# One stream for the recurrences of four token groups in a fused decoder block

## The chip, the core and the metric

The kernel runs on one core of a Trainium2 chip. A core has TensorE (PE; its weight loads are shown as PEld), VectorE (DVE), ScalarE (ACT), GpSimd (POOL) and a queue SP that issues the transfers here. Each works through its own instructions in order; semaphores tie them together. The metric is device time in microseconds for one execution; lower is better. Before the change the median of three runs is 2995.38 us.

## What is computed

One layer of a decoder on 2048 tokens of width 1024, in float32:

```python
u = rmsnorm(h, attn_pre_norm)
hq, hf, hi, hg, sq, sk, sv = split(u @ w_in)          # 7 parts of 512 columns
o_hg = rmsnorm(hgrn2_mix(hq, hf, hi, lb), hg_out_norm) * silu(hg)
o_sb = rmsnorm(stick_breaking_mix(sq, sk, sv), sb_out_norm)
h = h + rmsnorm(concat(o_hg, o_sb) @ w_out, attn_post_norm)
h = h + rmsnorm((silu(gate) * up) @ w_down, ffn_post_norm)   # gate, up from rmsnorm(h) @ w_gate_up
h = h + (p @ ple_proj) * sigmoid(h @ ple_gate)
```

`hgrn2_mix` is a gated linear recurrence with 4 heads: S_t = diag(f_t) S_(t-1) + (1 - f_t) v_t^T and o_t = S_t^T q_t, with a state of 128x128 per head. f comes from the logits `hf`, q from `hq` after silu, v is `hi`, and `hg` gates the output. `stick_breaking_mix` is strictly causal attention with 8 heads of width 64.

## The kernel before

The tokens are worked in four groups of 512 (`NG`, `GT`), each of four blocks of 128 (`TT`, `P`). Products that need more than one pass split both operands into a high and a low part and use three matmuls (`mm3`, L214 to L217).

**Two input projections per group.** `in_proj` (L335) computes either keys, queries and values of the attention (`KQV`, kind "a", 24 slots) or the four parts of the recurrence in the order hf, hq, hv, hg (`HG`, kind "b", 32 slots, eight for each part). A slot is two yields of the generator. Weights come through four raw buffers and a split (`weight`, L207; its DMA is L210, its subtraction L202). Results go to scratch in DRAM: `hf_s`, `hq_s`, `hv_s` and `hg_s` hold a group's logits, queries, values and gates (L367 to L381).

**The attention** is one stream for all groups (`attention`, L393), 320 units of two steps each. A unit makes scores into a `z` bank (L418), two sigmoids on ACT (L424, L425), a scan on DVE into `ring` (L439) and a product on POOL into `a` (L443). Four units later `a` is transposed (L451), split into `ah` (ACT, L454) and `al` (DVE, L456), and multiplied with the values (L467, L468).

**The recurrence** of one group is `hgrn(g)` (L501). For each of the four heads it has eleven steps, and two follow at the end, so 46 in all (`HG_STEPS`). A head's first step loads q (L508), logits z (L509), values v (L510) and gate (L511), makes pd and ks from z (L513 to L516), a tree of products on POOL (L524), and the first level. Seven level steps follow (`LEVELS`): matmuls into the bank `hg` (L533 for widths under 32, L544 for 32 and 64), a masked copy on DVE (L536), then a product of qp on POOL (L570) and one of ks on DVE (L572), both of which the next level needs. Then come a step that transposes ks (L577), one that multiplies it with v (L583) and forms the states on DVE (L587, sl in L593), and one that makes the output (L597, L598), adds its squares to `acc` on POOL (L605), multiplies with the gate (L606) and stores to `o_s` (L607). The last two steps sum `acc` over the head dimension with a matmul by ones (L613). There is one `hg` bank, and one buffer each for z, v, gate, pd, ks and qp; q has two. The state `hstate[h]` carries a head from group to group.

**What sets the order.** TensorE's order is the order of the program text, made by hand: `weave` (L51) advances a main stream slot by slot and steps the other streams as they fall due. The other engines and SP are ordered by a planner, which takes instructions by program order and its own estimate of when each becomes ready. `Rate` (L1181) deals out a number of steps of a stream over a number of slots. The phase says in which half of a slot steps are taken: 0, 1, or None for both.

The plan (L1221) lists seven projections that run after the first one: kind, group, units of attention, steps of recurrence. Before, each group's recurrence is a stream of its own, and an entry takes steps of one of them: n = 2 and 3 of group 0, n = 4 and 5 of group 1, n = 6 of group 2:

```python
("a", 1, units[0], 0), ("b", 0, 42, 0),
("a", 2, units[1] - 42, 21), ("b", 1, 48, 26),
("a", 3, 40, 21), ("b", 2, 52, 26), ("b", 3, 54, 42),
```

A group's recurrence is drained when n = 3 and n = 5 end. After n = 1 and n = 3 the last three slots are left to `in_u` (L306), which makes the operands of a later group and also uses the `hg` bank. Then come the output projections (`out_proj`, L642; 16 slots each). Beside that of group 0 run the last four steps of group 2 in the first two slots, and then group 3 at 46 steps over 30 slots, on into that of group 1. `out_load` (L620) loads a group's outputs from `o_s` for its output projection (DMA L625), and `post_mix` (L695) normalises and adds after it. The rest, a feed-forward with seven products in place of eight per block and the embedding gate, follows from about 1465 us on and is not touched.

Of the kernel before, what the change touches and what calls it, by code (L numbers as in the profile page):

```python
# [15 lines left out]
P = 128  # L16
# [74 lines left out]
def hybrid_block(  # L91
# [73 lines left out]
    def bank(tag):  # L165
        return ps.tile([P, 512], F32, tag=tag, name=tag, bufs=BANKS[tag])
# [334 lines left out]
    def hgrn(g):  # L501
        acc = None
        for h in range(HH):
# [6 lines left out]
            nc.sync.dma_start(v, hv_s[g][:, h * P:(h + 1) * P].rearrange("(c s) d -> s c d", s=P))  # L510
            nc.sync.dma_start(gate.rearrange("p c t -> p (c t)"), hg_s[g][h])  # L511
# [38 lines left out]
            for w in LEVELS:  # L550
                if w < BL:
                    level(qp, masks[w])
                else:
                    if w == BL:
                        b = bank("hg")
                        for i in range(0, P, BL):
                            nc.scalar.copy(score[i:i + BL, :, i:i + BL], small[i:i + BL])
                    blocks(b, w)
# [15 lines left out]
                yield  # L574
            kb = bank("hg")
# [15 lines left out]
            ob = bank("hg")  # L591
# [3 lines left out]
            yield  # L595
            for c in range(TT):
                nc.tensor.matmul(ob[:, c * P:(c + 1) * P], v[:, c, :], score[:, c, :], start=True, stop=False)  # L597
                nc.tensor.matmul(ob[:, c * P:(c + 1) * P], states[c], qp[:, c, :], start=False, stop=True)  # L598
# [597 lines left out]
    for i in range(WARM):  # L1196
# [26 lines left out]
        ("a", 2, units[1] - 42, 21), ("b", 1, 48, 26),  # L1223
        ("a", 3, 40, 21), ("b", 2, 52, 26), ("b", 3, 54, 42),
    ]
    hgs = [Stream(hgrn(g)) for g in range(NG)]
    spent = 0
    for n, (kind, g, att_n, hg_n) in enumerate(plan):
        slots = IN_A if kind == "a" else IN_B
        main = Stream(in_proj(g, us[g], KQV if kind == "a" else HG))  # L1230
        hg = {2: 0, 3: 0, 4: 1, 5: 1, 6: 2}.get(n)
        hg = hgs[hg] if hg is not None else idle
        tail = 3 if kind == "b" and g + 2 < NG else 0
        ra, rh = Rate(att_stream, 2, att_n, slots), Rate(hg, 1, hg_n, slots - tail)
        spent += att_n
        nxt = g + 2 if kind == "b" and g + 2 < NG else None
# [4 lines left out]
        if n in (3, 5):  # L1241
            hg.drain()
# [8 lines left out]
    r2 = Rate(hgs[2], 1, HG_STEPS - 42, 2)  # L1251
    r3 = Rate(hgs[3], 1, HG_STEPS, 2 * OP_SLOTS - 2)
# [9 lines left out]
    for g in range(NG - 1):  # L1262
# [3 lines left out]
        if g == 0:  # L1266
            weave(op, 2, rates.part(2), r2.part(2))
            hgs[2].drain()
            weave(op, OP_SLOTS - 2, rates.part(OP_SLOTS - 2), r3.part(OP_SLOTS - 2))
        elif g == 1:  # L1270
            weave(op, half, rates.part(half), r3.part(half), (pm, TT, 0))
            tu = Stream(turn(un_s[0], u_s[0], g_ffn, ["mm"], xt, ev))
            weave(op, half, rates.part(half), r3.part(half), (tu, 9, 0))
            hgs[3].drain()
# [95 lines left out]
```

## Time and profile before

| what | us |
|---|---|
| median of three runs (2991.2 to 3005.97) | 2995.38 |
| the profiled execution | 2993.67 |
| its span, first to last instruction | 2991.8 |
| TensorE busy in it | 2905.4 (97%) |
| first and last store of a recurrence head's output (L607) | 396.0, 1333.1 |
| DVE, ACT, POOL busy | 2067.2, 1581.7, 1404.1 |

The profile is of one execution. Busy time of an engine is the union of its instructions' times; matmuls are pipelined, so a busy TensorE is not one at its peak. "PE x <- DVE y" means that TensorE, at the instruction that writes x, waited for the DVE instruction that writes y. The granted clock (PEclk) is the share of the full TensorE clock; windows are in us from the span's start.

### The profile page before, as it was taken

How to read it: one execution, taken by the hardware profiler on the slowest of the kernel's cores; microseconds unless marked ns; L12 is line 12 of the kernel's file. 1: busy time of each engine (PE TensorE's matmuls, PEld its weight loads, DVE VectorE, ACT ScalarE, POOL GpSimd, SP SyncE). 2: the span in 40 equal slices, each digit the busy share in tenths (PEclk: the TensorE clock that was granted, in tenths of full speed). 3: DMA queues.
4: the chain of work that ended last, by engine and by line, in shares of the span. 5: the costliest groups of instructions: out<-in, count | busy, mean ns of one | idle time of the engine just before them, and what ended most of it. 6: DMA issues, size and time to landing. Idle time of an engine off the chain costs nothing.

```text
span 2991.8 us, 52684 instructions
## 1 busy us (share of the span) xinstructions
PE 2905.4 (97%) x18188; PEld 2424.4 (81%) x18188; DVE 2067.2 (69%) x2993; ACT 1581.7 (53%) x3182; POOL 1404.1 (47%) x1396
## 2 busy tenths in 40 slices
PE   9999999999999999898999999999999999999999
PEld 7788788878787887788878888788888888878777
DVE  3566667787777776766787787655877765656785
ACT  5666756676667666667533333455433323545542
POOL 3344556555556666765522211355622121456653
PEclk9999999999999999999999999999999999999999
DMA  7675665555445444457866787766965555677974
GB/s 223 206 221 156 181 183 165 147 175 165 142 138 162 148 134 133 158 189 260 288 185 209 252 289 259 244 206 209 346 201 163 166 176 176 208 218 234 326 250 162
DMA packets 469419, 602.27 MB, mean 201 GB/s; under 512 B 43168, under 2 KB 277664, under 8 KB 469152
## 3 DMA queue, kind: packets, MB, share of 16 engines
q1 hardware_dynamic: 469152, 598.91, 63.7%
q8 instruction: 143, 2.34, 0.3%
q14 instruction: 124, 1.02, 0.1%
HBM read 439.89 MB, written 158.86 MB: 200 GB/s over the span
## 4 chain that ended last, share of the span: by engine, by line
PE 47%; DMA 4%; POOL 3%; issue 3%; DVE 2%; ACT 1%; SPq 0%; POOLq 0%; ACTq 0%; DVEq 0%
PE mm L215 6%; PE mm L217 6%; PE mm L216 6%; PE z L217 4%; PE z L215 4%; PE z L216 4%; PE av L216 2%; PE av L215 2%; PE av L217 2%; PE tr L215 2%; PE tr L217 2%; PE tr L216 2%; POOL c L828 1%; POOL wl L821 1%; PE hg L217 1%
## 5 line engine op out<-in xcount | busy, mean ns | idle before, releaser
L820 ACT CAST wh<-wr 128x512 fp32r<-128x512 f32 x600 | 351.4, 618 | 477.3 <-PE mm L216 186.2
L821 POOL TENSOR_TENSOR wl<-wr,wh 128x512 fp32r<-128x512 f32 x256 | 366.9, 1440 | 471.5 <-ACT wh L820 416.8
L443 POOL TENSOR_TENSOR a<-be,ring 128x512 f32<-128x512 f32 (+2 forms) x320 | 320.0, 1000 | 417.1 <-DVE ring L439 394.4
L215 PE MATMUL mm<-uh,wh 128*128 128x512 f32 x1168 | 480.9, 412 | 3.5 <-DVE vv L358 2.4
L216 PE MATMUL mm<-ul,wh 128*128 128x512 f32 x1168 | 459.0, 393 | 3.9 <-DVE ul L821 2.3
L217 PE MATMUL mm<-uh,wl 128*128 128x512 f32 x1168 | 460.2, 394 | 0.0
L821 DVE TENSOR_TENSOR wl<-wr,wh 128x512 fp32r<-128x512 f32 x344 | 301.1, 883 | 183.9 <-ACT wh L820 173.3
L439 DVE TENSOR_TENSOR_SCAN ring<-z,ring,be 128x512 f32<-128x512 f32 x192 | 245.7, 1279 | 106.3 <-ACT z L425 103.8
L215 PE MATMUL mm<-wh,uh 128*128 128x256 f32 (+1 forms) x992 | 307.3, 310 | 0.9 <-DVE vv L358 0.9
L216 PE MATMUL mm<-wl,uh 128*128 128x256 f32 (+1 forms) x992 | 293.6, 296 | 0.6 <-POOL wl L821 0.6
L217 PE MATMUL mm<-wh,ul 128*128 128x256 f32 (+1 forms) x992 | 293.6, 296 | 0.0
L217 PEld LDWEIGHTS mm<-uh,wl 128*128 128x128 f32 x1168 | 220.4, 189 | 50.7
L215 PEld LDWEIGHTS mm<-uh,wh 128*128 128x128 f32 x1168 | 221.2, 189 | 46.2 <-issue 2.6
L216 PEld LDWEIGHTS mm<-ul,wh 128*128 128x128 f32 x1168 | 221.6, 190 | 44.8 <-DVE ul L821 2.7
L201 ACT CAST wh<-wr 128x512 fp32r<-128x512 f32 x288 | 178.3, 620 | 124.4 <-PE mm L216 71.7
L202 POOL TENSOR_TENSOR wl<-wr,wh 128x512 fp32r<-128x512 f32 x144 | 190.1, 1320 | 101.6 <-ACT wh L201 97.0
L424 ACT ACTIVATE be<-z 128x512 f32<-128x512 f32 (+2 forms) x320 | 171.0, 534 | 114.2 <-DVE z L422 66.8
L456 DVE TENSOR_TENSOR al<-tr,ah 128x512 fp32r<-128x512 f32 (+1 forms) x320 | 191.8, 599 | 50.5 <-ACT ah L454 48.6
L821 POOL TENSOR_TENSOR wl<-s,wh 128x512 fp32r<-128x512 f32 x44 | 73.0, 1661 | 300.7 <-ACT wh L820 263.6
L454 ACT CAST ah<-tr 128x512 fp32r<-128x512 f32 (+1 forms) x320 | 167.7, 524 | 87.8 <-PE tr L451 85.1
L215 PEld LDWEIGHTS mm<-wh,uh 128*128 128x128 f32 x992 | 191.4, 193 | 9.2 <-issue 1.1
L216 PEld LDWEIGHTS mm<-wl,uh 128*128 128x128 f32 x992 | 191.8, 193 | 6.5 <-POOL wl L821 1.1
(315 smaller groups left out, 7190.0 us busy)
## 6 DMA issues: line engine op xcount, KB each, us to landing
wr<-in_w_gate_up_dram SPq DMA_DIRECT2D x308, 256.0 KB, 3.8
wr<-in_w_in_dram SPq DMA_DIRECT2D x224, 256.0 KB, 3.2
wr<-hid_s SPq DMA_DIRECT2D x154, 256.0 KB, 3.3
wr<-in_w_down_dram SPq DMA_DIRECT2D x110, 256.0 KB, 3.6
wr<-wd_s SPq DMA_DIRECT2D x88, 256.0 KB, 3.2
kt<-k_s SPq DMA_DIRECT2D x80, 256.0 KB, 3.2
vt<-v_s SPq DMA_DIRECT2D x80, 256.0 KB, 3.4
wr<-h_s SPq DMA_DIRECT2D x80, 256.0 KB, 4.4
```

Of the source, the lines that this page charges most:

```text
L201: nc.scalar.copy(hi, src)
L202: (lo_engine or nc.gpsimd).tensor_tensor(lo, src, hi.bitcast(F32), op=ALU.subtract)
L215: nc.tensor.matmul(o, l[0], r[0], start=start, stop=False)
L216: nc.tensor.matmul(o, l[0], r[1], start=False, stop=False)
L217: nc.tensor.matmul(o, l[1], r[0], start=False, stop=stop)
L424: nc.scalar.activation(be[:, :n], z[:, :n], AF.Sigmoid, scale=0.125)
L439: nc.vector.tensor_tensor_scan(r[:, o:o + n][:, ::-1], z[:, :n][:, ::-1], be[:, :n][:, ::-1], init, op0=ALU.mult, op1=ALU.bypass)
L443: nc.gpsimd.tensor_tensor(a[:, :n], be[:, :n], r[:, o + 1:o + n + 1], op=ALU.mult)
L454: nc.scalar.copy(hi[:, lo_c:], tr[:, lo_c:])
L456: nc.vector.tensor_tensor(lo[:, lo_c:], tr[:, lo_c:], hi[:, lo_c:].bitcast(F32), op=ALU.subtract)
L820: nc.scalar.copy(hi, src)
L821: lo_engine.tensor_tensor(lo, src, hi.bitcast(F32), op=ALU.subtract)
```

## The change

The four streams become one, `hg`, that runs through the groups in order, 184 steps. The plan's entries take 24, 30, 20, 28 and 40 steps of it (142), wherever in the groups they fall, and the other 42 are dealt out over all 32 slots of the output projections of groups 0 and 1. So group 1 begins in n = 3, group 2 in n = 5 and group 3 at the end of n = 6, each while the projection that makes its own inputs is still under way. Within `hgrn`, the load of the values moves from the head's first step to the level of width 32 (its seventh step), and that of the gate to the step that transposes ks (its ninth); both now stand in the text behind the stores that they read. The bank for the output `ob` is asked for in the step that uses it. The entry n = 2 takes its steps in both halves of a slot (24 steps in 24 slots), n = 3 still in the second half alone. The drains after n = 3 and n = 5 go.

```diff
@@ -507,8 +507,6 @@
             q, z, v, gate = ht("q", 2), ht("z"), ht("v"), ht("gate")
             nc.sync.dma_start(q.rearrange("p c t -> p (c t)"), hq_s[g][h])
             nc.sync.dma_start(z.rearrange("p c t -> p (c t)"), hf_s[g][h])
-            nc.sync.dma_start(v, hv_s[g][:, h * P:(h + 1) * P].rearrange("(c s) d -> s c d", s=P))
-            nc.sync.dma_start(gate.rearrange("p c t -> p (c t)"), hg_s[g][h])
             pd, ks, qp = ht("pd"), ht("ks"), ht("qp")
             nc.scalar.activation(pd, z, AF.Sigmoid)
             nc.scalar.activation(ks, z, AF.Sigmoid, scale=-1.0)
@@ -552,6 +550,7 @@
                     level(qp, masks[w])
                 else:
                     if w == BL:
+                        nc.sync.dma_start(v, hv_s[g][:, h * P:(h + 1) * P].rearrange("(c s) d -> s c d", s=P))
                         b = bank("hg")
                         for i in range(0, P, BL):
                             nc.scalar.copy(score[i:i + BL, :, i:i + BL], small[i:i + BL])
@@ -572,6 +571,7 @@
                 nc.vector.tensor_tensor(
                     kv[:, :, 0, :], kv[:, :, 0, :], pv[:, :, 1:2].to_broadcast((P, n, w)), op=ALU.mult)
                 yield
+            nc.sync.dma_start(gate.rearrange("p c t -> p (c t)"), hg_s[g][h])
             kb = bank("hg")
             for c in range(TT):
                 nc.tensor.transpose(kb[:, c * P:(c + 1) * P], ks[:, c, :], ident)
@@ -588,11 +588,11 @@
                     st[:, c, :], states[-1], last[:, c:c + 1], sbk[:, c * P:(c + 1) * P],
                     op0=ALU.mult, op1=ALU.add)
                 states.append(st[:, c, :])
-            ob = bank("hg")
             s_last = ht("sl", shape=(P, P))
             nc.vector.scalar_tensor_tensor(
                 s_last, states[-1], last[:, TT - 1:TT], sbk[:, (TT - 1) * P:], op0=ALU.mult, op1=ALU.add)
             yield
+            ob = bank("hg")
             for c in range(TT):
                 nc.tensor.matmul(ob[:, c * P:(c + 1) * P], v[:, c, :], score[:, c, :], start=True, stop=False)
                 nc.tensor.matmul(ob[:, c * P:(c + 1) * P], states[c], qp[:, c, :], start=False, stop=True)
@@ -1220,26 +1220,23 @@
 
     plan = [
         ("a", 1, units[0], 0), ("b", 0, 42, 0),
-        ("a", 2, units[1] - 42, 21), ("b", 1, 48, 26),
-        ("a", 3, 40, 21), ("b", 2, 52, 26), ("b", 3, 54, 42),
+        ("a", 2, units[1] - 42, 24), ("b", 1, 48, 30),
+        ("a", 3, 40, 20), ("b", 2, 52, 28), ("b", 3, 54, 40),
     ]
-    hgs = [Stream(hgrn(g)) for g in range(NG)]
-    spent = 0
+    hg = Stream(st for g in range(NG) for st in hgrn(g))
+    spent = hg_spent = 0
     for n, (kind, g, att_n, hg_n) in enumerate(plan):
         slots = IN_A if kind == "a" else IN_B
         main = Stream(in_proj(g, us[g], KQV if kind == "a" else HG))
-        hg = {2: 0, 3: 0, 4: 1, 5: 1, 6: 2}.get(n)
-        hg = hgs[hg] if hg is not None else idle
         tail = 3 if kind == "b" and g + 2 < NG else 0
         ra, rh = Rate(att_stream, 2, att_n, slots), Rate(hg, 1, hg_n, slots - tail)
         spent += att_n
+        hg_spent += hg_n
         nxt = g + 2 if kind == "b" and g + 2 < NG else None
         toks = in_norm(nxt) if nxt else []
         if n == 6:
             out_load(0, res[0])
         weave(main, slots - tail, ra.part(slots - tail), rh.part(slots - tail, 1 if hg_n < slots else None))
-        if n in (3, 5):
-            hg.drain()
         if nxt:
             un = Stream(in_u(toks, us[nxt], ["hg", "mm"]))
             weave(main, tail, ra.part(tail), (un, 2 * tail, 0))
@@ -1248,8 +1245,7 @@
         main.drain()
     todo = total_units - spent + LAG + 1
     rates = Rate(att_stream, 2, todo, 2 * OP_SLOTS)
-    r2 = Rate(hgs[2], 1, HG_STEPS - 42, 2)
-    r3 = Rate(hgs[3], 1, HG_STEPS, 2 * OP_SLOTS - 2)
+    rh = Rate(hg, 1, NG * HG_STEPS - hg_spent, 2 * OP_SLOTS)
     half = OP_SLOTS // 2
     tt0, tt1, ss0, ss1 = {}, {}, {}, {}
 
@@ -1264,14 +1260,12 @@
             out_load(g + 1, res[g + 1])
         op = Stream(out_proj(g, res[g]))
         if g == 0:
-            weave(op, 2, rates.part(2), r2.part(2))
-            hgs[2].drain()
-            weave(op, OP_SLOTS - 2, rates.part(OP_SLOTS - 2), r3.part(OP_SLOTS - 2))
+            weave(op, OP_SLOTS, rates.part(OP_SLOTS), rh.part(OP_SLOTS))
         elif g == 1:
-            weave(op, half, rates.part(half), r3.part(half), (pm, TT, 0))
+            weave(op, half, rates.part(half), rh.part(half), (pm, TT, 0))
             tu = Stream(turn(un_s[0], u_s[0], g_ffn, ["mm"], xt, ev))
-            weave(op, half, rates.part(half), r3.part(half), (tu, 9, 0))
-            hgs[3].drain()
+            weave(op, half, rates.part(half), rh.part(half), (tu, 9, 0))
+            hg.drain()
             att_stream.drain()
             side.close()
             big[0] = ctx.enter_context(tc.tile_pool(name="bigr", bufs=1, side="right"))
```

## The prediction

> **What bounds the kernel now.** I read the page's busy times first, then a table of busy time by stage, then who keeps TensorE waiting, then the granted clock stretch by stretch.
>
> ```profile
> span 2991.8 us, 52684 instructions
> PE 2905.4 (97%) x18188; PEld 2424.4 (81%) x18188; DVE 2067.2 (69%) x2993; ACT 1581.7 (53%) x3182; POOL 1404.1 (47%) x1396
> core 0: us, PE busy (x) PEld busy (x) DVE busy (x) ACT busy (x) POOL busy (x), PEclk, DMA share, GB/s
> 342.00:462.00 120.00, 118.34 (x1116) 101.26 (x1114) 81.16 (x137) 76.83 (x164) 65.52 (x82) 1.00 0.64 192
> 462.00:622.00 160.00, 159.08 (x1287) 134.20 (x1286) 118.45 (x174) 110.18 (x233) 88.11 (x112) 1.00 0.51 152
> 622.00:765.00 143.00, 139.34 (x1195) 115.68 (x1194) 109.03 (x169) 95.59 (x209) 78.78 (x101) 1.00 0.57 164
> 765.00:942.00 177.00, 172.53 (x1389) 142.62 (x1388) 130.79 (x181) 120.32 (x251) 105.34 (x125) 1.00 0.50 146
> 942.00:1139.00 197.00, 189.88 (x1805) 154.09 (x1805) 144.65 (x216) 133.28 (x281) 123.95 (x149) 0.99 0.48 143
> 1139.00:1240.00 101.00, 91.96 (x1038) 82.67 (x1037) 73.02 (x119) 64.29 (x141) 69.48 (x85) 0.97 0.41 129
> 1240.00:1340.00 100.00, 92.97 (x1048) 83.85 (x1047) 63.74 (x103) 67.28 (x148) 67.64 (x77) 0.95 0.57 186
> ```
>
> The seven rows are the stages that the change touches, in order: entries n = 2, 3, 4, 5, 6 of the plan, then the output projections of groups 0 and 1. TensorE sets the end almost everywhere (97%), so a reordering can win only what TensorE loses. Length minus its busy time is 1.66, 0.92, 3.66, 4.47, 7.12, 9.04 and 7.03 us, 33.9 us in all. The last two stages have the largest share, and the clock falls below 1.00 there. In these two run 50 recurrence steps in 32 slots (1.56 per slot); entry n = 6 has 42 in 32 (1.31), n = 2 to 5 have 21/24, 25/32, 21/24 and 25/32 (0.78 to 0.88; a stream has 46 steps, so the last request of 26 finds 25).
>
> Who holds TensorE up, in the two output-projection stages (first seven rows), in n = 6 (next row) and in n = 2 to 5 together (last):
>
> ```profile
> PE av L468 <- DVE al L456: 5.8, 3, 4.1
> PE hg L533 <- POOL qp L570: 2.8, 3, 1.8
> PE hg L597 <- DVE sl L593: 2.5, 3, 1.1
> PE av L467 <- ACT ah L454: 1.5, 2, 1.0
> PE hg L613 <- POOL acc L605: 1.4, 1, 1.4
> PE hg L533 <- DVE ks L572: 1.0, 2, 0.7
> PE hg L544 <- POOL ring L433: 0.9, 1, 0.9
> ...
> PE hg L533 <- POOL qp L570: 0.8, 1, 0.8
> ...
> PE hg L533 <- DVE ul L327: 1.7, 1, 1.7
> ```
>
> The columns are total us, times, longest. Where steps run at 1.56 per slot, waits of the recurrence (bank `hg`) are 2.8 + 2.5 + 1.4 + 1.0 + 0.9 = 8.6 us; at 1.31 they are 0.8 us; at the lower rates 1.7 us over 600 us, and no DMA stands in any of these lists. The other half of the waits at the end is the attention's (5.8 + 1.5 us).
>
> The clock: five stalls and what follows each (timeline of TensorE with its idle time in brackets, then the five stretches after them).
>
> ```profile
> 1133.33 0.51 PE L467 MATMUL av<-ah,vt 128*128 128x512 f32 x1 [2.49 <-ACT ah L454]
> 1150.45 1.06 PE L613 MATMUL hg<-ones,acc 128*128 128x1 f32 x8 [1.35 <-POOL acc L605]
> 1236.58 0.71 PE L468 MATMUL av<-al,vt 128*128 128x512 f32 x1 [4.13 <-DVE al L456]
> 1253.18 0.46 PE L533 MATMUL hg<-qp,ks 128*32 128x32 f32 x32 [1.78 <-POOL qp L570]
> 1271.05 0.47 PE L468 MATMUL av<-al,vt 128*128 128x128 f32 x1 [1.30 <-DVE al L456]
> ...
> 1134.30:1137.70 3.40, 3.40 (x10) 2.83 (x11) 1.24 (x2) 2.67 (x6) 0.64 (x1) 0.50 0.45 152
> 1148.00:1151.40 3.40, 2.05 (x17) 1.68 (x15) 1.69 (x4) 3.27 (x7) 2.98 (x4) 0.99 0.38 141
> 1151.40:1154.80 3.40, 3.40 (x15) 3.30 (x16) 0.95 (x2) 0.72 (x4) 3.40 (x4) 0.50 0.85 275
> 1236.70:1240.10 3.40, 3.40 (x16) 3.22 (x17) 3.40 (x5) 3.06 (x9) 2.76 (x5) 0.50 0.73 225
> 1253.80:1257.20 3.40, 3.40 (x14) 2.68 (x13) 1.81 (x3) 1.52 (x5) 3.40 (x3) 0.50 0.48 167
> 1270.80:1277.70 6.90, 6.65 (x44) 5.48 (x44) 3.06 (x6) 6.30 (x16) 4.18 (x7) 0.51 0.49 167
> ```
>
> After each stall the clock is 0.50 for 3.4 us (6.9 after the last), so a stall also costs half of what follows: 1.7 us, or 3.4. Two of the five (1150, 1253) are the recurrence's; the other three wait for the attention's operands ah and al.
>
> The Trainium skill (TensorE: Matmul & The Clock Gate, Part 1: The HAM clock gate) says that the clock is halved after at least one idle window of about 3.4 us. Here the window before 1151.40 was busy for 2.05 of 3.40 us and the clock halved all the same, so the row decides. By the page's rule, read strictly, the stall at 1150 would be worth only its own 1.35 us, 1.7 us less than the sum below has for it.
>
> **The change part by part.** (a) *The squeezed end of group 2.* Before, its last four steps stand in the first two slots of the first output projection, two per slot, so the sum of squares (L605, POOL) and the matmul that reads it (L613) follow each other too closely: the stall at 1150. After, 24 + 30 + 20 + 28 = 102 steps are done ahead of n = 6, so group 2 ends at its step 138, which is 36 of the 40 of n = 6, at 1.25 per slot. The ends of groups 0 and 1, at lower rates, show no such wait. Gone: 1.35 + 1.7 = 3.05 us.
>
> (b) *The rest of the recurrence's waits in the two last stages*, 8.6 - 1.4 = 7.2 us, and 1.7 us of half clock after 1253: 8.9 us. The rate falls from 1.56 to 42/32 = 1.31. From the one side, waits in proportion to the rate fall by 16%: 1.4 us. From the other, n = 6 had exactly 42 steps in 32 slots and 0.8 us: 8.1 us gone. But the mix normalisation and the loads of the next group's outputs go on at these places and not much in n = 6, so neither row is nearer; I take 4.5 us.
>
> (c) *Steps moved earlier.* Ten steps leave (8 here, 2 from n = 6); one leaves n = 4 and 11 come into n = 2 (+3), n = 3 (+5) and n = 5 (+3). TensorE's own work for a step is
>
> ```profile
> 942.00:1139.00 197.00, 27.21 (x926) 22.94 (x927) 12.87 (x38) 7.66 (x19) 0.99 0.48 143
> ```
>
> on bank `hg` in n = 6 (the first column after the length is TensorE's busy time): 27.21 / 42 = 0.65 us. That work is moved and not saved: nil. Waits that it brings: at most what the denser n = 6 shows over n = 5, (7.12 - 4.47) us for 17 more steps, 0.16 us each, 1.6 us for ten; at least nothing. The rates stay at or below 1.0 per slot, but the phase in n = 2 changes too. I take 1.5 us. Cover gone would mean the price of n = 6 throughout, which is this bound.
>
> (d) *Values and gate loaded later, a group begun while its projections run.* What the engines beside TensorE do is not tied to the place in the program:
>
> ```profile
> L509 SPq DMA_DIRECT2D z<-hf_s x16: 319/338/537, 214.7 to 1226.6; - x16
> L533 PE MATMUL hg<-q,ks x512: 189/196/218, 344.1 to 1295.9; 128*32 128x32 f32 x171
> L510 SPq DMA_DIRECT2D v<-hv_s x16: 359/371/802, 284.8 to 1291.9; - x16
> DMA to landing us min/median/max: 2.8/3.3/3.8
> SPq L510 <- PE hg L598: 17.4, 10, 2.7
> SPq L511 <- DMA o_s<-gate: 14.7, 11, 2.4
> SPq L210 <- POOL wl L202: 202.0, 88, 8.1
> ```
>
> The first head's logits are loaded at 214.7 us and its values at 284.8, its first matmul is at 344.1: the planner already issues loads long ahead, as soon as the source is stored and the buffer free. So a group's early start changes TensorE's order alone. The moved loads cost as many descriptors as before (two per head). They now may wait less: at most 17.4 + 14.7 = 32.1 us of SP's blocked time goes. Behind those waits on SP stand weight, key and value loads, but TensorE waits for no DMA in these stages, so I put it at nil. Their loss, if they come late instead, is a rival below. The bank for `ob` is asked for after the yield: there is one `hg` bank, its matmul waits for sl (L593) either way: nil.
>
> Sum: -3.05 - 4.5 + 1.5 = -6 us. The profiled run took 2993.67 us (span 2991.8 and 1.9 around it), which gives 2987.6; the runs' median, 2995.38, is 1.7 above it, so **2989 us**. With the ends of (b) and (c) the forecast alone runs from 2995.4 - 11.2 = 2984 to 2995.4 - 2.9 = 2993.
>
> **Rivals.** *The last stages become like n = 6.* Stalls of the attention's ah and al share ACT, DVE and POOL queues with the recurrence; if easing these queues removes them too, the 201 us lose 7.12/197 of their length as n = 6 does, 7.3 us, instead of 9.04 + 7.03 + half of 17.1 us at half clock (1151, 1236, 1253, 1270) = 24.6: a gain of 17.3, 2978 us. For: POOL is busy for 69% and 68% there against 63% in n = 6. Against: eight steps of 50 are a small part of these queues' work, and those three stalls come as the next group's outputs are loaded, which is unchanged.
>
> *The waits move and nothing is won.* ACT, DVE and POOL run in order, in the order of a planner that works from estimates; a new order makes new near misses of the kind of 1133 or 1236. One such is 2.5 to 4.1 us and 1.7 of clock; one or two of them eat the 6 us: 2995 us. For: three of five stalls are of that kind now.
>
> *The moved loads come late: slower.* Gate is issued in the text two steps ahead of its use (L606), values three ahead of theirs (L583). A step of n = 6 lasts 197/42 = 4.7 us, so gate has 9.4 us. An SP queue blocked for its longest 8.1 us and 3.3 us of transfer make 11.4: two us late. L606 then holds DVE, behind it al and the scans, and TensorE stalls and loses the clock: 2 + 1.7 = 3.7 us a head, up to 4.13 + 1.7 = 5.8. With two of 16 heads late the gain is gone; six give 22 - 6 = 16 us over, 3011 us. For: these loads lose their early place in the program. Against: first loads issued 60 to 130 us ahead.
>
> *It does less than it says:* the new rates are 1.0, 0.94, 0.83, 0.88, 1.25 and 1.31 per slot, not even; that is in the sum already.
>
> **How the numbers follow.** About 0.5% (15 us) is what a measurement of this kernel tells from no change: below 2980.4 or above 3010.4. Chances: forecast 0.46, like n = 6 0.20, nothing won 0.22, late loads 0.12. The second gives most of "faster" (0.18), the lower edge of the forecast with the runs' spread (2991 to 3006) 0.08: 0.26. Late loads give 0.08 of "slower" and unlucky order 0.04: 0.12. The rest, 0.62, is no change. The range takes the second rival with a few us more of spread, 2972, and reaches to half of the late heads, 3008; the likeliest alone, with the runs' spread, 2980 to 3000.
>
> **What would show it.** (a) right: no L613 wait and no half clock in the first 15 us of the first output projection. (b) right: waits of `hg` lines in the output projections together about 4 us; wrong if 7 or more, or 1 or less. (c) wrong if TensorE loses over 3 us more in n = 2 to 5 than the 10.7 us now. (d) wrong if TensorE waits at L583 or after L606, or SP's waits at the moved loads last longer than now. The whole is wrong if the three stalls on ah and al vanish, or multiply.

## The result, and the profile after

The kernel after takes 3019.85 us (median; 3014.26 to 3026.04), the kernel before, run beside it, 2995.25 us (2991.2 to 3005.97). The ratio is 1.0073, with a 95% interval of 1.0057 to 1.0088: slower by 0.73%, which is beyond the half per cent that a measurement tells from no change, on the other side of the forecast of 2989 us and above the range's upper end of 3008 us. In a later set of runs the same kernel gave 1.0057 (1.0036 to 1.0078).

The head of the page after, span and busy time of each engine:

```profile
span 3023.9 us, 52683 instructions
PE 2920.3 (97%) x18188; PEld 2436.4 (81%) x18188; DVE 2078.7 (69%) x2993; ACT 1581.0 (52%) x3182; POOL 1397.1 (46%) x1396
```

The work is the same, TensorE's 18188 matmuls included. To see where the time went I cut both traces at the same matmuls of the main products, so that a stage holds the same main work in both. "tail" is the last slots of n = 1 with `in_u`; op0 to op3 are the output projections of groups 0 to 3. A stage begins at the third of its main matmuls, so a wait just ahead of that counts in the stage before: the first recurrence step of n = 2 lies in "tail", and the sums at the start of op0 and op1 (L649) lie in n6 and op0. Length of each stage, us; the second row of each kernel is a second profiled execution:

| | tail | n2 | n3 | n4 | n5 | n6 | op0 | op1 | op2 | op3 | sum | remaining part |
|---|---|---|---|---|---|---|---|---|---|---|---|---|
| before | 19.5 | 118.4 | 158.9 | 142.8 | 178.4 | 197.2 | 101.2 | 98.8 | 59.4 | 65.0 | 1139.6 | 1526.7 |
| before, again | 20.0 | 118.3 | 158.9 | 142.8 | 178.7 | 196.0 | 101.5 | 97.5 | 58.8 | 65.6 | 1138.1 | 1535.0 |
| after | 23.9 | 123.3 | 161.1 | 144.8 | 181.5 | 200.8 | 98.1 | 99.4 | 64.7 | 63.8 | 1161.4 | 1537.2 |
| after, again | 24.3 | 123.3 | 161.1 | 144.9 | 180.5 | 199.3 | 95.7 | 97.1 | 65.1 | 66.1 | 1157.3 | 1530.5 |

The remaining part (feed-forward and embedding gate, where the text is the same) varies by 8 us between two executions of one kernel, so it is left out of the reading; the ten stages before it grew by 18 to 23 us, about what the ratios of the two sets give (17 and 25 us). The first profile of before happened to have a short remaining part.

Busy time by stage after, tail first and then n2 to op2 (columns as in the prediction's table):

```profile
325.32:349.25 23.93, 19.34 (x126) 15.85 (x124) 14.06 (x25) 19.81 (x46) 9.15 (x14) 0.86 0.62 198
349.25:472.51 123.26, 120.91 (x1242) 102.38 (x1240) 82.56 (x142) 71.86 (x150) 66.58 (x82) 1.00 0.62 176
472.51:633.59 161.08, 160.34 (x1341) 135.25 (x1339) 119.59 (x176) 111.10 (x240) 89.17 (x115) 1.00 0.50 151
633.59:778.42 144.83, 139.60 (x1186) 115.04 (x1185) 110.60 (x167) 94.17 (x204) 77.94 (x101) 1.00 0.58 167
778.42:959.96 181.54, 176.72 (x1430) 146.31 (x1429) 132.99 (x187) 123.78 (x259) 108.63 (x134) 1.00 0.50 145
959.96:1160.75 200.79, 189.23 (x1757) 153.75 (x1756) 143.47 (x219) 131.39 (x275) 123.83 (x149) 0.99 0.48 145
1160.75:1258.81 98.06, 87.84 (x979) 78.94 (x979) 68.77 (x108) 62.55 (x138) 65.09 (x78) 0.94 0.40 124
1258.81:1358.24 99.43, 92.21 (x909) 84.50 (x909) 64.74 (x93) 66.93 (x147) 58.41 (x68) 0.91 0.55 179
1358.24:1422.98 64.74, 53.99 (x395) 52.65 (x393) 40.17 (x51) 41.38 (x91) 37.15 (x36) 0.89 0.71 234
```

The first of these and the last, of the kernel before, cut at the same matmuls:

```profile
325.55:345.08 19.53, 17.05 (x126) 13.80 (x125) 13.47 (x24) 15.19 (x35) 6.62 (x9) 1.00 0.68 213
1340.79:1400.17 59.38, 50.71 (x395) 49.57 (x394) 39.12 (x51) 42.75 (x94) 37.89 (x36) 0.94 0.77 259
```

Three things stand out. The tail grew by 4.4 us, with a clock of 0.86 in place of 1.00. n = 2 to 5 grew as steps came in, but the two stages that lost eight steps got little shorter, and their clock fell from 0.97 and 0.95 to 0.94 and 0.91. And op2, in which no step of the recurrence stands, grew by 5.4 us.

Who holds TensorE up after, in the two output projections (the view that the prediction quotes for before):

```profile
PE tr L649 <- DVE al L456: 7.5, 1, 7.5
PE av L468 <- DVE al L456: 7.1, 4, 4.0
PE av L467 <- ACT ah L454: 1.3, 1, 1.3
PE hg L542 <- DVE ks L571: 0.7, 1, 0.7
PE hg L597 <- DVE sl L592: 0.5, 1, 0.5
PE hg L531 <- POOL ring L433: 0.2, 1, 0.2
```

The waits on bank `hg` fell from 8.6 us to 1.4. The attention's, on ah and al, rose from 7.3 us to 15.9, with one stall of 7.5 us that before did not have, at the matmul that sums the squares of the attention's outputs at the start of op1 (L649). The same matmul at the start of op0, which by these cuts lies in n6, waits 3.1 us, against 0.2 us before.

### The profile page after: what moved, and what is told of

Read it like the earlier page. It is cut to its first block, busy times and chain, and to the rows that moved or that the text cites. A ratio compares the mean times of both kernels' runs of the same rounds, so it can differ in the third digit from the quotient of the medians.

```text
span 3023.9 us, 52683 instructions
## 1 busy us (share of the span) xinstructions
PE 2920.3 (97%) x18188; PEld 2436.4 (81%) x18188; DVE 2078.7 (69%) x2993; ACT 1581.0 (52%) x3182; POOL 1397.1 (46%) x1396
## 5 line engine op out<-in xcount | busy, mean ns | idle before, releaser
L456 DVE TENSOR_TENSOR al<-tr,ah 128x512 fp32r<-128x512 f32 (+1 forms) x320 | 192.0, 600 | 59.3 <-ACT ah L454 57.4
L216 PEld LDWEIGHTS mm<-wl,uh 128*128 128x128 f32 x992 | 193.8, 195 | 7.1 <-POOL wl L821 1.4
```

The costliest lines, as they stand in the source:

```text
L216: nc.tensor.matmul(o, l[0], r[1], start=False, stop=False)
L456: nc.vector.tensor_tensor(lo[:, lo_c:], tr[:, lo_c:], hi[:, lo_c:].bitcast(F32), op=ALU.subtract)
```

## The experiments

Five theories stood against each other. Theory 1: the new order of TensorE meets bursts of work on ACT and DVE at three places (the start of n = 2, of n = 6 and of op1). Theory 2: the difference is chance in one execution. Theory 3: steps taken earlier simply cost more. Theory 4: any new order makes the planner draw its near misses anew. Theory 5, formed on the way: the output projections are held at their start by the burst of loading a group's outputs (`out_load`: L625, L630) together with the mix normalisation (L706, L707). In the kernel after, some lines of `hgrn` have other numbers: L533, L544, L570, L572 and L593 of before are L531, L542, L569, L571 and L592, and the loads of values and gate are L553 and L574.

In all of the experiments the stage table is read beside the ratio, since a stage shows a few us that the ratio's interval hides. The names e1 to e13 are those that the expectations use.

| | tail | n2 to n5 | n6 | op0 + op1 | op2 | sum of ten | ratio to before |
|---|---|---|---|---|---|---|---|
| before (two executions) | 19.5, 20.0 | 598.5, 598.7 | 197.2, 196.0 | 200.0, 199.0 | 59.4, 58.8 | 1139.6, 1138.1 | 0.9995 (0.9983 to 1.0007) |
| after, again | 24.3 | 609.7 | 199.3 | 192.8 | 65.1 | 1157.3 | 1.0057 (1.0036 to 1.0078) |
| e1: after, n = 2 in the second half | 19.0 | 608.6 | 199.7 | 189.8 | 66.6 | 1145.0 | 1.0032 (1.0016 to 1.0049) |
| e2: before, loads later | 19.1 | 598.5 | 196.6 | 199.0 | 58.7 | 1134.6 | 0.9996 (0.9980 to 1.0011) |
| e3: before, n = 2 from the first half | 24.3 | 599.3 | 198.0 | 199.0 | 59.7 | 1144.6 | 1.0019 (1.0002 to 1.0036) |
| e4: relief alone | 19.5 | 599.6 | 207.9 | 191.5 | 64.8 | 1147.0 | 1.0045 (1.0032 to 1.0057) |
| e5: early steps alone | 18.9 | 608.0 | 195.8 | 198.1 | 59.6 | 1147.3 | 1.0033 (1.0021 to 1.0046) |
| e6: before, end of group 2 | 18.7 | 598.0 | 205.9 | 201.2 | 61.9 | 1151.1 | 1.0054 (1.0041 to 1.0067) |
| e7: neighbouring deal | 20.3 | 610.8 | 198.8 | 190.1 | 61.2 | 1146.7 | 1.0036 (1.0020 to 1.0052) |
| e8: output loads in the middle | 19.1 | 608.5 | 193.1 | 190.6 | 66.5 | 1143.3 | 1.0016 (1.0004 to 1.0028) |
| e9: before, output loads in the middle | 19.7 | 597.9 | 197.6 | 200.2 | 59.5 | 1139.9 | 1.0010 (0.9999 to 1.0022) |
| e10: no steps in op1 | 19.5 | 609.8 | 203.6 | 207.0 | 61.6 | 1167.8 | 1.0106 (1.0083 to 1.0129) |
| e11: weights first | 19.0 | 610.2 | 193.8 | 188.9 | 63.9 | 1141.6 | 1.0015 (0.9998 to 1.0031) |
| e12: before, weights first | 18.9 | 598.0 | 198.2 | 200.6 | 59.5 | 1139.9 | 1.0004 (0.9990 to 1.0019) |
| e13: neighbouring deal, loads in the middle | 19.1 | 609.3 | 194.6 | 193.2 | 64.4 | 1144.1 | 1.0013 (0.9997 to 1.0030) |

### Both kernels again

No edit, the kernel after:

> The changed kernel as it is, profiled a second time. Theory 1 (TensorE's new order meets bursts of ACT and DVE work at three places: the start of n = 2, the start of n = 6, the start of the second output projection): the stalls of 4.2 us at 343, 1.2 to 1.5 us at 950 to 971 and 7.5, 2.5 and 4.0 us at 1256 to 1293 stand at the same places again, and the time is 3015 to 3025. Theory 2 (chance of one execution): other places and sizes. The halved clock at 1888, in code that is not touched, is expected to be missing.

And, beside a later set of runs, the kernel before against itself:

> The kernel before, profiled a second time: which of its stalls stand again, and how long the code after 1465 us takes (1526.7 us in the first profile, 1529 to 1539 in the profiles of the other kernels, whose code there is the same). Expected: the stalls at the same places within 0.5 us, and 1527 to 1535 us behind them.

The loss came back (1.0057, 3014 us) with the same stages: tail 24.3, n2 123.3, op2 65.1, and the same stall at L649 (7.4 us); the halved clock at 1888 is gone. The kernel before against itself is 0.9995; its largest stalls stand again (4.1 and then 4.3 us at L468, but 2.5 and then 1.6 us at 1133). Theory 2 falls.

### The start of n = 2

Edit of the kernel after (e1): the steps of n = 2 in the second half of a slot, as before.

```diff
-rh.part(slots - tail, 1 if hg_n < slots else None)
+rh.part(slots - tail, 1 if n == 2 or hg_n < slots else None)
```

> The changed kernel with the steps of n = 2 taken in the second half of a slot, as before. Theory 1: TensorE then works through one half slot ahead of the first recurrence step, the wait for ul at its start falls from 4.2 to about 1.7 us as before and its 6.8 us at half clock go: 2.5 + 3.4 = 6 us won, 3014. Theory 3 (steps that come earlier simply cost more there, whatever their place in a slot): 3020, no change.

The other way round, in the kernel before: its 21 steps of n = 2 from the first half on.

```diff
-rh.part(slots - tail, 1 if hg_n < slots else None)
+rh.part(slots - tail, 1 if n != 2 and hg_n < slots else None)
```

> The kernel before, with its 21 steps of n = 2 taken in both halves of a slot, so that the first comes in the first half. Theory 1: the wait at the first step grows from 1.7 to about 4.2 us and the clock halves for 3.4 to 6.8 us: 2995 + 4 to 6 = 3000. Theory 3: the number of steps is that of before, so 2995.

The first matmul of the recurrence in the timeline of TensorE, for before, after, the first edit and the second:

```profile
344.11 0.46 PE L533 MATMUL hg<-q,ks 128*32 128x32 f32 x32 [1.66 <-DVE ul L327]
```

```profile
343.43 0.66 PE L531 MATMUL hg<-q,ks 128*32 128x32 f32 x32 [4.20 <-DVE ul L327]
```

```profile
344.07 0.46 PE L531 MATMUL hg<-q,ks 128*32 128x32 f32 x32 [1.66 <-DVE ul L327]
```

```profile
345.82 0.40 PE L533 MATMUL hg<-q,ks 128*32 128x32 f32 x13 [4.20 <-DVE ul L327]
```

`in_u` ends with transposes into bank `hg` (L310), which DVE has to read (L327) before the bank is free. With steps in the first half, the first step stands directly behind these transposes and waits 4.20 us; in the second half, six matmuls of the main product, two of the attention and its transposes stand between, and the wait is 1.66 us. What follows, in the kernel after:

```profile
338.80:342.30 3.50, 0.43 (x3) 0.12 (x2) 2.37 (x5) 3.50 (x9) 0.86 (x2) 1.00 0.59 174
342.30:345.70 3.40, 2.27 (x36) 1.95 (x37) 2.70 (x5) 3.37 (x8) 0.81 (x1) 0.51 0.97 333
345.70:349.20 3.50, 3.50 (x11) 2.82 (x11) 0.00 (x0) 3.44 (x9) 1.77 (x5) 0.51 0.07 27
```

The clock is halved for 6.9 us, about 3.4 us of work. The edit that takes the first half away brings the tail from 24 to 19.0 us and the ratio from 1.0057 to 1.0032; the edit that puts the first half into the kernel before brings its tail from 19.5 to 24.3 and costs 0.19% (0.02 to 0.36). So this place is shown in both directions: about 5 us by the tail, a part of the loss but not all of it.

### The loads alone

Edit of the kernel before: only the loads of values and gate, and the request for `ob`, as in the change.

> The kernel before, with only the loads of values and gates moved to the seventh and ninth step and the bank for the output asked for later; TensorE's order is that of before. Late loads (the rival on record) would show here: 3.7 to 5.8 us for each head that they hold, up to 3011. Theories 1 and 3: TensorE's order alone counts, 2995, within 5 us.

0.9996, and the stages that the change touches are as before. The loads land where they did: in the kernel after the first values are issued at 284.5 us, against 284.8 before, and TensorE has no wait at L583.

```profile
L553 SPq DMA_DIRECT2D v<-hv_s x16: 359/373/585, 284.5 to 1302.6; - x16
...
SPq L553 <- PE hg L598: 17.5, 11, 4.2
SPq L574 <- DMA o_s<-gate: 17.3, 7, 5.2
```

The rival of the late loads falls.

### The two halves of the deal

The steps of n = 2 to 5 nearly as before, and only the output projections relieved (on the kernel after with n = 2 in the second half):

```diff
-("a", 2, units[1] - 42, 24), ("b", 1, 48, 30),
-("a", 3, 40, 20), ("b", 2, 52, 28), ("b", 3, 54, 40),
+("a", 2, units[1] - 42, 21), ("b", 1, 48, 25),
+("a", 3, 40, 21), ("b", 2, 52, 25), ("b", 3, 54, 50),
```

> One stream, but entries n = 2 to 5 take 21, 25, 21 and 25 steps as before and n = 6 takes 50, so that 42 are left for the output projections of groups 0 and 1; nothing moves into n = 2 to 5. Theory 1 (the output projections do win as forecast, the loss is made ahead of them): the two together last about 190 us as in the changed kernel (200.0 before), n = 2 to 5 last as before, n = 6 gets 8 x 0.65 = 5.2 us of work and a few us of waits; in all 2 us under to 3 us over before. Theory 3 (a step moved earlier costs more than it saves, most where steps are dense): n = 6 at 1.56 steps per slot loses as the output projections did, 10 us or more; 5 to 10 us over before.

The early steps as in the change, the output projections at 50 steps as before (on the same kernel):

```diff
-("a", 3, 40, 20), ("b", 2, 52, 28), ("b", 3, 54, 40),
+("a", 3, 40, 20), ("b", 2, 52, 28), ("b", 3, 54, 32),
```

> One stream with 24, 30, 20 and 28 steps in n = 2 to 5 (n = 2 in the second half of a slot) but only 32 in n = 6, so that 50 steps stay in the output projections of groups 0 and 1, as many as before. Theory 1: the early moves cost what e1 shows beyond the moved work in n = 2 to 5, about 10.1 - 10 x 0.65 = 4 us, n = 6 gives its 10 steps back, the output projections win nothing: 4 us over before. Theory 3: the same or more, 4 to 8. If the time is that of before, the loss is in n = 6 and after.

Both halves lose, 0.45% and 0.33%, and they don't add up to the 0.32% of both together. The relief shortens op0 and op1 by 8 us, 5.2 us of it moved work (8 steps of 0.65), but n = 6 pays 10.7 us for 8 more steps, where the work alone is 5.2, and op2 pays 5.4. In the other, n = 2 to 5 pay 9.5 us for ten more steps (6.5 of work), and n = 6, ten steps lighter, gives back 1.4 us at most: its busy time falls by 5.5 us, from 189.9 to 184.4, and its idle time rises from 7.3 to 11.4. Of the forecasts, theory 1's failed in both (at most 3 and 4 us over before; about 13 and 10 were measured). Theory 3 came nearer: it named 10 us or more for n = 6 in the first, but its totals, 5 to 10 and 4 to 8 us, are short too, and it doesn't say why op2 should grow.

### The end of group 2 alone

Edit of the kernel before: the last four steps of group 2 into n = 6, group 3 over all 32 slots.

```diff
-("a", 3, 40, 21), ("b", 2, 52, 26), ("b", 3, 54, 42),
+("a", 3, 40, 21), ("b", 2, 52, 26), ("b", 3, 54, 46),
...
-r2 = Rate(hgs[2], 1, HG_STEPS - 42, 2)
-r3 = Rate(hgs[3], 1, HG_STEPS, 2 * OP_SLOTS - 2)
+r3 = Rate(hgs[3], 1, HG_STEPS, 2 * OP_SLOTS)
```

> The kernel before with all 46 steps of group 2 in n = 6 and group 3's 46 over all 32 slots of the two output projections: the squeezed end of group 2 goes, nothing else. My step (a): the wait at L613 of 1.35 us and the 3.4 us at half clock after it go, 3 us won. Theory 4 (the stall is only replaced: the planner's new order of the other engines brings another near miss): no change, within 3 us of before.

The wait at L613 is gone, as step (a) said, and the kernel is slower by 0.54%. In the two output projections TensorE now waits

```profile
PE mm L755 <- DMA xt<-un_s: 7.8, 1, 7.8
PE tr L649 <- DVE al L456: 5.9, 2, 3.8
PE av L468 <- DVE al L456: 2.8, 3, 1.7
PE hg L533 <- POOL qp L570: 2.2, 3, 1.3
```

and n = 6 is 8.7 us longer for four steps, 2.6 us of work (2.1 us of it is the wait at L649 that starts op0). The stall that went was 1.35 us. Both forecasts missed: step (a) said 3 us won, theory 4 no change within 3 us. This is the clearest sign that a wait taken away at a place that many engines share need not be a gain: n6, op0 and op1 hold the same work in this kernel and in before, and take 407.1 us against 397.2.

### A neighbouring deal

On the kernel with n = 2 in the second half: 23, 31, 21, 27, 40 in place of 24, 30, 20, 28, 40.

> As e1 (the changed kernel with the second half of the slot in n = 2), with one step moved between neighbours: 23, 31, 21, 27, 40. Theory 1 and 3 (a systematic cost): the same as e1, 0.3% over before, within 3 us; the third output projection lasts 65 to 67 us as in e1 (59 before). Theory 4 (the planner's order and its near misses decide, each new order draws anew): another sum, over 4 us from e1, and a third output projection of another length.

The time is the same (1.0036 and 1.0032), but made up otherwise: n3 is 4.0 us longer (165.1 against 161.1) for one more step, and op2 is 5.4 us shorter (61.2 against 66.6), though neither has a step of the recurrence in op2 and TensorE's order is the same there. Each theory is half right here. Single stages moved by 4 to 5 us in either sense for a shift of one step, op2 among them, as theory 4 has it and theories 1 and 3 do not; but the sum hardly moved (1146.7 against 1145.0), where theory 4 named over 4 us.

### The stall at the start of op1

What stands before the stall of 7.5 us in the kernel after, in the timelines of TensorE and of DVE:

```profile
1256.54 1.84 PE L649 MATMUL tr<-ones,oss 128*128 128x1 f32 x8 [7.52 <-DVE al L456]
```

```profile
1246.95 0.68 DVE L456 TENSOR_TENSOR al<-tr,ah 128x512 fp32r<-128x512 f32 x1
1247.55 2.41 DVE L706 SCALAR_TENSOR_TENSOR mix<-mix,rstd,gb 128x512 f32<-128x512 f32 x2
1249.88 0.29 DVE L422 TENSOR_TENSOR z<-z,maskneg 128x128 f32<-128x128 f32 x1
1250.09 1.76 DVE L630 SCALAR_TENSOR_TENSOR ul<-tmp,g_sb,uh 128x512 fp32r<-128x512 f32 x1
1251.77 0.63 DVE L651 COPY rg<-hgss 128x4 f32<-128x4 f32 x1
1252.31 0.68 DVE L202 TENSOR_TENSOR wl<-wr,wh 128x512 fp32r<-128x512 f32 x1
1252.91 1.74 DVE L630 SCALAR_TENSOR_TENSOR ul<-tmp,g_sb,uh 128x512 fp32r<-128x512 f32 x1
1254.58 0.68 DVE L707 TENSOR_TENSOR h<-h,mix 128x512 f32<-128x512 f32 x1
1255.18 0.29 DVE L534 COPY_PREDICATED small<-mask,hg 128x128 f32<-128x128 uint8 x1
1255.38 0.41 DVE L571 TENSOR_TENSOR ks<-ks,tree 128x256 f32<-128x256 f32 x1
1255.71 0.68 DVE L456 TENSOR_TENSOR al<-tr,ah 128x512 fp32r<-128x512 f32 x1
```

L649 needs the bank `tr`, which the attention's transposes filled and al (L456) frees. DVE is never idle here; al starts at 1255.71, 8.1 us after the al before it ended, because in DVE's order it stands behind the mix normalisation (L706, L707: 3.1 us), two products of the next group's outputs (L630: 3.5 us) and two small operations of the recurrence (L534, L571: 0.7 us). Those two products took 1.76 and 1.74 us, where the median of the kernel's sixteen is 0.75 us; why they were slower here was not tested. The recurrence's own operations are little of what delays al. What follows the stall is at half clock:

```profile
1257.10:1264.00 6.90, 6.90 (x59) 6.19 (x60) 4.28 (x8) 4.68 (x11) 6.34 (x8) 0.50 0.68 227
```

To test theory 5, the calls that load the outputs were moved from the start of n = 6, op0 and op1 to half-way through them, on the kernel with n = 2 in the second half:

```diff
...
 if g == 0:
-    weave(op, OP_SLOTS, rates.part(OP_SLOTS), rh.part(OP_SLOTS))
+    weave(op, half, rates.part(half), rh.part(half))
+    out_load(1, res[1])
+    weave(op, half, rates.part(half), rh.part(half))
 elif g == 1:
     weave(op, half, rates.part(half), rh.part(half), (pm, TT, 0))
+    out_load(2, res[2])
```

> As e1, with the loading of a group's outputs (tmp from o_s, its split on ACT, DVE and POOL) moved from the start of n = 6 and of the output projections of groups 0 and 1 to the middle of these stages. Theory 5 (the output projections are held at their start by a burst on ACT and DVE, the loads of the next group's outputs together with the mix normalisation; taking recurrence steps away only makes TensorE wait for it at another instruction): the waits of 3.1 and 7.5 us for al at the two sums (L649) go to under 1.5 us each, the half clock after them too: some 10 us won on e1, if the loads find room in the middle; 0 to 0.1% under before. Theory 4 (near misses drawn anew by each order): waits of the same size elsewhere, 0.3% over before as e1.

and in the same way on the kernel before:

> The kernel before with the same move of the loading of outputs to the middle of n = 6 and of the two output projections; the recurrence as before. Theory 5: the waits of 2.5 us at 1133 and 4.1 us at 1236 and the half clock after them go, 6 to 10 us won on before (0.2 to 0.3%). Theory 4: within 3 us of before.

In the first, L649's stall in op1 falls from 7.53 us to

```profile
1238.15 1.84 PE L649 MATMUL tr<-ones,oss 128*128 128x1 f32 x8 [3.91 <-DVE al L456]
```

and the one at the start of op0 from 3.08 to 0.66 us, with which n6 falls from 199.7 to 193.1 us. Theory 5 had both under 1.5 us and some 10 us won. The ratio is 1.0016 after 1.0032, with intervals that overlap; the ten stages together are only 1.6 us shorter, since op3 and op1 grew. So a gain is likely and its size is open. On the kernel before, where theory 5 had 6 to 10 us won, nothing that can be measured changed (1.0010, 0.9999 to 1.0022). The wait of 4.13 us for al stands there as it did:

```profile
1233.48 0.79 PE L468 MATMUL av<-al,vt 128*128 128x512 f32 x1 [4.59 <-DVE al L456]
```

But the edit does less than it was meant to. It moves the call, and the planner still runs the first two of a group's four products (L630) where it did. On the kernel before, two run ahead of the al that is waited for either way, at 1231.5 and 1234.8 us in before and at 1228.2 and 1230.7 with the edit, so that run doesn't test theory 5. On the kernel of e1 three ran ahead of L649 in op1 (1235.5, 1240.0, 1242.9), and with the edit two do (1232.8, 1235.0; 2.0 us together), while the others follow at 1264.7 and 1265.7. A load less ahead of al and a shorter wait agree with theory 5; but al now also stands ahead of the mix normalisation, so they can't be told from a new draw of the planner's. If the recurrence had no share in it at all, taking all its steps out of op1 would leave it (on the kernel of e1):

```diff
-rh = Rate(hg, 1, NG * HG_STEPS - hg_spent, 2 * OP_SLOTS)
+rh = Rate(hg, 1, NG * HG_STEPS - hg_spent, OP_SLOTS)
```

> As e1, but the 42 steps of the output projections all in that of group 0 (2.6 per slot) and none in that of group 1. It asks for the start of the second output projection alone, the time is of no interest (over before). Theory 5: the wait for al at the second L649 stays above 5 us with no recurrence step beside it, since the burst is not the recurrence's. If the recurrence's share of DVE and POOL makes it, it falls under 3 us.

L649 then waits 2.24 us and the attention's matmul ahead of it 2.35, 4.6 together against 7.5, with al again behind products of L630 and L707. By the expectation this speaks against theory 5: the wait at L649 was to stay above 5 us, and under 3 us meant the recurrence's share. That the queue still holds TensorE for 4.6 us with no step beside it says that the recurrence is not all of it either; with op0 filled by 42 steps the order ahead is another one, so the shares stay open. With 42 steps in the 16 slots of op0, that stage takes 126.6 us and the kernel loses 1.06% (two runs); waits of `hg` there are 6.3 + 3.5 + 3.1 + 1.8 us and more, so a squeeze of the recurrence is dear, as step (b) had it; only the relief from it was not.

### op2

TensorE waits there for the low and high parts of weights. Before, and after:

```profile
PE z L216 <- POOL wl L202: 8.7, 4, 4.3
```

```profile
PE z L216 <- POOL wl L202: 7.5, 3, 3.4
PE z L215 <- ACT wh L201: 1.3, 1, 1.3
PE av L215 <- ACT wh L201: 1.1, 1, 1.1
PE av L216 <- POOL wl L202: 1.0, 1, 1.0
```

So I gave the weights of this projection precedence with the planner, on the kernel with the outputs' loads in the middle:

```diff
-ws = [weight(w_cols(kk)) for kk in range(0, HH, 2)]
+with tc.high_priority() if first else nullcontext():
+    ws = [weight(w_cols(kk)) for kk in range(0, HH, 2)]
```

> As e8, with the weights of the third output projection (no recurrence step runs beside it) given priority in the planner's order. That stage lasts 64.7 to 66.6 us in the changed kernel, e1, e4 and e8, 58.7 to 59.7 us in before and its repeats, 61.2 us in e7, with the same order on TensorE. Theory 4 for this stage (the planner places weight loads and their splits behind other work there): back to 60 us or less, about 6 us won on e8, level with before. If the stage stays at 65 us, the cause is not the place of the weights in the queues.

and on the kernel before:

> The kernel before with the same priority for the weights of the third output projection. Theory 4: the stage (59.4 us) loses part of its 8.7 us of waits for weights and lasts 53 to 58 us; up to 5 us won. If the stage stays at 59 or grows, weights behind other work are not what it waits for in before.

On the first, op2 went from 66.5 to 63.9 us, not to 60, and the time stayed (1.0016 and, on another chip, 1.0015). On the kernel before nothing changed (59.5 us, 1.0004), and this run is no test: the loads of weights (L210) stand where they stood, 2.9, 3.9, 13.6, 21.0 and 29.5 us after the stage's start against 2.9, 4.0, 13.9, 20.9 and 29.4. Last, the neighbouring deal together with the outputs' loads in the middle:

> As e8 (loads of outputs in the middle, second half of the slot in n = 2) with the deal of e7: 23, 31, 21, 27, 40. Theory 4: the third output projection is drawn anew, 61 us as in e7 or 66 as in e8, and the sum of n = 2 to the second output projection stays within 3 us of e8; 0 to 0.2% over before.

op2 is 64.4 us, neither of the two lengths named, and n = 2 to op1 together take 5 us more than in e8, where theory 4 had at most 3; the ratio, 1.0013, is in its range. So neither precedence of the weights nor the deal settles op2; what the runs show is that op2 takes 58.7 to 59.7 us in every kernel with 50 steps in op0 and op1, and 61.2 to 66.6 in those with 46 or 42. Whether a choice of the planner does it, or TensorE only comes earlier to weights that are ready no sooner, no run here separates. For the second speaks that op0 to op2 together take 259.4 and 257.8 us in before, and 257.9 in after again, 256.4 in e1, 256.3 in e4 and 257.1 in e8; against it, 251.3 in e7. No version here is faster than before.

## Why the prediction was wrong

The step that failed is (b), on which the sum rested: the recurrence's waits went as forecast, and the time they cost was not won. An estimate by stages, with a moved step put at 0.83 us (below), has after lose against before 4 us in the tail, 4 in n = 2 to 5, 5 in n = 6, 4 in op0 and op1 and 5 in op2, so no one place carries the loss. The steps in turn:

(a) *The squeezed end of group 2, -3.05 us.* The wait at L613 is gone, in the kernel after and in the experiment that moves that end alone. But what would show it was also no half clock in the first 15 us of the first output projection, and after has 6.9 us of it right at its start, behind a stall of 3.1 us at L649 on al:

```profile
1154.80:1158.10 3.30, 0.60 (x34) 0.35 (x32) 3.30 (x6) 1.41 (x4) 2.51 (x3) 1.00 0.58 178
1158.10:1165.00 6.90, 6.52 (x56) 5.84 (x57) 2.43 (x7) 3.31 (x6) 4.63 (x5) 0.51 0.23 74
```

By itself the edit costs 0.54% on the kernel before. The step failed: a stall was taken away, and the time was not won.

(b) *The rest of the recurrence's waits, -4.5 us (-1.4 to -8.1).* The `hg` waits in op0 and op1 fell to 1.4 us, and to 0.7 us with n = 2 in the second half, which is more than I took, and below the 1 us that I had named as a sign that the step is wrong. But TensorE's idle time in the two stages (length minus busy) went from 8.86 + 7.03 = 15.9 us to 10.22 + 7.22 = 17.4, and to 14.6 with n = 2 in the second half. I priced the waits by their name and took the rest of the two stages as fixed; the same DVE and ACT queues serve the attention, and TensorE now waits there, 15.9 us where it was 7.3. This is the rival "the waits move and nothing is won", which I gave 0.22: one or two new near misses of 2.5 to 4.1 us and 1.7 us of clock. It came nearest, with one miss of 7.5 us and 6.9 us of half clock behind it in place of 4.1 and 3.4.

(c) *Steps moved earlier, +1.5 us (0 to 1.6).* TensorE's own work is zero-sum, as said: with n = 2 in the second half, busy time in n2 to n5 rose by 8.3 us (ten more steps, 0.8 us each and not the 0.65 of their matmuls on `hg` alone) and in n6, op0 and op1 fell by 9.9. The waits were mis-sized. I noted that the phase of n = 2 changes and then priced it by the rate, as if a step waited the same wherever it stands in a slot; the first step behind `in_u`'s transposes waits 4.20 us for the bank and not 1.66, and halves the clock: about 5 us, outside the step's bound, shown in both directions. (Its rate for n = 3, 30/32, also leaves out the three slots kept for `in_u`: it is 30 steps in 29 slots, 1.03.) In n2 to n5 idle time rose from 9.05 us to 13.1 (10.8 with n = 2 in the second half), over the 3 us that I had named as the sign of an error, and n6, with two steps fewer, rose from 7.30 to 11.56, of which 2.9 are the wait at L649 that starts op0.

(d) *Later loads, nil.* Right in the time: 0.9996 for that part alone, and TensorE waits neither at L583 nor after L606 in after. But the sign named for an error did show: SP's wait for the gate's load behind the head's store grew from 14.7 us (longest 2.4) to 17.3 (5.2). That wait cost nothing in the kernel with the later loads alone, where it is 17.2 us (3.3), so it was no sign of a loss.

Not in the sum at all was op2, 5 to 6 us in both executions of after. I had read the stages up to the last one that holds a step, and what the change does to the order of the other engines does not end there.

Why is after outside my range? Its upper end, 3008 us, came from the late heads, a mechanism that did not occur (half of six, three heads at 3.7 to 5.8 us each, would give 3000 to 3007 by the prediction's own sum), and the rival of moved waits was held at one or two near misses that cancel the gain. The loss of the second set of runs is 17 us (1.0057). By the ratios 7.5 us of it go with n = 2 in the second half (1.0032; about 5 by the tail), 4.8 more with the outputs' loads in the middle (1.0016; 1.6 by the ten stages), and 4.8 are left (its interval: 1 to 8); neighbouring intervals overlap, and only the first part is also shown by its stage, in both directions. The first set's 24.6 us (1.0073) is 7 us more; the two intervals overlap. For the first part the cause is shown, by taking it away and by putting it into the kernel before. For the others the places are shown (n6, L649, op2); that they are redrawn near misses is argued from the neighbouring deal, and not shown.

## What to carry to other kernels

Waits counted under one name need not be a gain to be had: where several streams share in-order engines, ask what TensorE reaches next when a wait goes, and whether its operand is any earlier. Before moving steps, look at which buffer the first moved step needs and who used it last; a change of half a slot there cost as much as everything else that the prediction summed. And on a kernel that is 97% busy, where other engines are ordered by a planner, set a few us of new waits against a new order of TensorE, in stages behind the changed ones too, before counting what the order saves: every kernel here that moved recurrence steps measured 0.1 to 1.1% above before, two of them (e11, e13) with intervals that reach down to it.

## What was not expected of the hardware

The clock is halved after windows that are partly busy, and the amount of work in them seems to decide: the stretches of 3.4 us just before a halving were busy for 0.43 us (338.8), 0.60 us (1154.8) and, in this row, 1.55 us, while the window at 1151.4 with 2.82 us busy was not followed by one.

```profile
1151.40:1154.80 3.40, 2.82 (x14) 1.88 (x12) 3.35 (x7) 3.39 (x9) 0.64 (x1) 1.00 0.43 151
...
1274.20:1277.60 3.40, 1.55 (x11) 1.09 (x9) 3.40 (x5) 3.31 (x10) 1.64 (x1) 1.00 0.23 67
1277.60:1284.40 6.80, 6.16 (x28) 5.45 (x29) 3.28 (x6) 3.60 (x13) 3.36 (x6) 0.50 0.42 142
```

The Trainium skill (TensorE: Matmul & The Clock Gate, Part 1: The HAM clock gate) asks for an idle window; none of these was idle, so here the rows decide. Cut into stretches of 3.4 us at the times at which the clock changes, the 17 profiles of this case hold, between 200 and 2900 us, 120 stretches at full clock with TensorE busy for under 1.5 us: every one was followed by half clock. Of those with 2.5 us or more none was, and between 1.5 and 2.5 us both occur, so work for about half of the stretch is the border. A stall of 1.4 to 4.2 us so costs 1.7 to 3.4 us on top, half of the 3.4 to 6.9 us at half clock. And the part of the program that no edit touches took between 1527 and 1543 us over the profiled executions, half a per cent of the whole, so a difference of that size between two single profiles is no evidence about a change.
